# RG-LRU branch of a hybrid decoder block: convolution read from PSUM, gelu projections ahead of the gates, weights rounded on ScalarE

## The chip, the cores and the metric

One core of one Trainium2 chip runs the whole kernel. The metric is device time in microseconds (us) of one execution; less is better. Engines are called PE (TensorE), DVE (VectorE), ACT (ScalarE), POOL (GpSimd) and SP (SyncE, which issues DMAs). PEld is PE's weight load.

## The reference

A decoder block over 512 tokens plus 16 learned meta tokens (528 in all), width 1024, float32. Cut to what matters here, it is:

```python
proj = rmsnorm(h, norm1_g) @ w_in            # columns for q, f, i, og, lx, ly, ga, gb
o_a = hgrn2_branch(q_pre, f_pre, i_pre, og_pre, lb, hg_norm_g)

# rglru_branch(lx, ly, ...), 1024 channels in 8 blocks of 128
xc = causal_depthwise_conv(lx, conv_w, width=4) + conv_b
r = sigmoid(xc_block @ w_r[block] + b_r)
i = sigmoid(xc_block @ w_i[block] + b_i)
log_a = -8 * r * softplus(-lam)
u = sqrt(-expm1(2 * log_a)) * (i * xc)
h_t = exp(log_a_t) * h_{t-1} + u_t           # scan over the tokens
o_b = h * gelu(ly)

merged = sigmoid(ga) * (o_a @ w_up_a) + sigmoid(gb) * (o_b @ w_up_b)
h = h + merged @ w_out
h = h + hier_moe(rmsnorm(h))                 # 32 experts, top-1 group, top-2 in it
return rmsnorm(h)[:, 16:]
```

The four taps of the convolution run over tokens: output token t takes lx of t, t-1, t-2 and t-3.

## The kernel before, in words

Channels lie on partitions and tokens along the free dimension. Every dense product is made of three matmuls of rounded operands: a float32 operand is split into a rounded high part (hi) and the rounded rest (lo), and the product is hi x hi + hi x lo + lo x hi. `split` (lines 85 to 90) does this: one engine copies with rounding (hi), another subtracts (lo).

**Weights.** The class `Weights` (lines 132 to 176) holds a queue of weight pieces in the order in which PE wants them (lines 178 to 193). A DMA of SP brings 256 columns (`raw`), `prep` rounds 128 of them into one of three buffers (`hl`), and `next` hands a piece to PE. Which engines round it is fixed where the piece is queued: for w_in's columns of lx (2048 on), ly (3072 on) and the gate blocks w_r and w_i, hi is made by DVE and lo by POOL; for the heads before it hi is made by ACT. `dense` (line 195) runs one projection in eight steps of k and calls `prep` in its middle for the piece after.

**The stage.** `lru` (line 619) goes over the eight blocks in four pairs. For a pair it projects lx for both blocks (`proj(True, ...)`, two PSUM tiles of 256 and 272 tokens each), and `use_lx` makes of each: two ACT copies from PSUM into `lxp` in SBUF (one buffer for all blocks), on DVE the fourth tap with the bias (line 639) and three more taps (line 641) into `xc`, then hi on ACT and lo on DVE into `xh` (one buffer). Then for each block of the pair `gates` (twelve matmuls into four PSUM tiles, tanh on ACT, products on DVE) and the block's ly projection with gelu (`use_ly`, into the tile `ge`, one buffer for both blocks of a pair).

**The finish.** `finish` of a pair (line 682: logarithms and exponentials on ACT, the scan over tokens and products on DVE, the rounding of o_b into `obH` on DVE and `obL` on POOL) is called after the next pair's lx projections; the last one is called at the end.

**What sets the order.** The program's text, then a scheduler that may hoist independent instructions on each engine; each engine then works through its own list in order and waits at the head of it. Eight PSUM banks are handed out by that scheduler as they come free. Beside the stage run the steps of the HGRN2 heads 2 and 3 (`hgrn_head`, one step after every fifth step of k): masks, exponentials and small matmuls. After the stage comes `merge` (line 788): for each of four column groups two gate projections (ga), two products with w_up_a, two gate projections (gb), two products with w_up_b, which need `obH` and `obL`; its weights are rounded by DVE and POOL. Buffers that come free in `merge` and after it start the DMAs of the expert weights (`prefetch`, line 747), which go on to the end.

Of the kernel before, what the change touches and what calls it, by code (L numbers as in the profile page):

```python
# [8 lines left out]
F32 = mybir.dt.float32  # L9
F32R = mybir.dt.float32r  # L10
# [4 lines left out]
AF = mybir.ActivationFunctionType  # L15
OP = mybir.AluOpType
# [4 lines left out]
N = T + M  # L21
D = 1024
KD = D // 128
# [5 lines left out]
EPS = 1e-6  # L29
BIG = 3.0e38  # L30
PARTS = ((0, 256), (256, 528))
NLATE = 10
EV1, EV2 = 2, 5
LEVELS = (64, 32, 16, 8, 4, 2, 1)
# [3 lines left out]
def hybrid_block_kernel(ctx: ExitStack, tc: tile.TileContext, x, meta, norm1_g, w_in, hg_lb,  # L38
# [37 lines left out]
    def ms(tag, shape, dtype, name):  # L76
        return misc.tile(shape, dtype, name=uniq(name), tag="m" + tag)

    def ps(shape, name, dtype=F32):
        return psum.tile(shape, dtype, name=name, tag="ps")  # L80
# [97 lines left out]
    W = Weights()  # L178
# [1 line left out]
        for base in (512, 0, 1024, 1536):  # L180
            W.columns(w_in2, base + 128 * h, ACT, POOL)
    for b in range(0, NB, 2):
        W.columns(w_in2, 2048 + 128 * b, DVE, POOL)
        W.blocks([w_r[0], w_i[0]], b, DVE, POOL)
        W.columns(w_in2, 3072 + 128 * b, DVE, POOL)
    for j in range(0, KD, 2):
        W.columns(w_in2, 4096 + 128 * j, DVE, POOL)
        if j:
# [6 lines left out]
    def dense(outs, cols_, nk, aH, aL):  # L195

        wh, wl = W.next()
        for k in range(nk):
            if k == nk // 2:
                W.prep()  # L200
            for w, a in ((wh, aH), (wh, aL), (wl, aH)):
                for o, (c0, c1) in zip(outs, cols_):
                    PE.matmul(o[:, :c1 - c0], w[:, k, :], hsl(a, k, c0, c1),  # L203
                              start=(k == 0 and w is wh and a is aH),
                              stop=(k == nk - 1 and w is wl))
            yield

    def proj(all_tokens, use):
        if all_tokens:
            pp = [ps([128, 272], "pj") for _ in PARTS]  # L210
            yield from dense(pp, PARTS, KD, hnH, hnL)
            use(pp)
        else:
            p_ = ps([128, 512], "pj")
            yield from dense([p_], [(M, N)], KD, hnH, hnL)
            use(p_)
# [119 lines left out]
    def col(nm, i=None):  # L336
        a, b = R[nm]
        return cols[:, a:b] if i is None else cols[:, a + i:a + i + 1]
# [278 lines left out]
        add_slots(late, [f"t{i}" for i in range(NLATE)])  # L617

    def lru():
        MX = ms("F", [128, 2, 3 + N], F32, "lxi")  # L620
        lxp, iv = MX[:, 0], MX[:, 1, :N]
        L2 = ms("G", [128, 2, N], F32, "l2")
        DVE.memset(lxp[:, :3], 0.0)
        tail = None
        for b0 in range(0, NB, 2):
            bs = (b0, b0 + 1)
            XC = ms("AH"[b0 // 2 % 2], [128, 2, N], F32, "xc")
            RR = ms("C", [128, 2, N], F32, "r")
            TH = ms("D", [128, 2, N], F32, "th")
            GE = ms("E", [128, 2, T], F32, "ge")  # L630
            XH = {}
            WG = []

            def use_lx(b):
                def f(pp):
                    for (a, c), p_ in zip(PARTS, pp):
                        ACT.activation(lxp[:, 3 + a:3 + c], p_[:, :c - a], AF.Copy)
                    xc = XC[:, b - b0]
                    DVE.tensor_scalar(xc, lxp[:, 3:], col("cw", 24 + b), col("cb", b), op0=OP.mult, op1=OP.add)
                    for w in range(3):  # L640
                        DVE.scalar_tensor_tensor(xc, lxp[:, w:w + N], col("cw", 8 * w + b), xc,  # L641
                                                 op0=OP.mult, op1=OP.add)
                    xh = XH[b] = ms("B", [128, 2, N], F32R, "xh")
                    split(xh[:, 0], xh[:, 1], xc, ACT, DVE)
                return f

            def gates(b):
                xh, i = XH[b], b - b0
                r, th = RR[:, i], TH[:, i]
                for gi, dst in enumerate((r, iv)):  # L650
                    pg = [ps([128, 272], "pg") for _ in PARTS]
                    for w, a in ((0, 0), (0, 1), (1, 0)):
                        for (c0, c1), p_ in zip(PARTS, pg):
                            PE.matmul(p_[:, :c1 - c0], WG[w][:, 2 * gi + i], xh[:, a, c0:c1], start=(w == 0 and a == 0), stop=(w == 1))
                    for (c0, c1), p_ in zip(PARTS, pg):
                        ACT.activation(dst[:, c0:c1], p_[:, :c1 - c0], AF.Tanh, scale=0.5, bias=hb[:, 8 * gi + b:8 * gi + b + 1])
                ACT.activation(th, r, AF.Tanh, scale=C4[:, b:b + 1], bias=C4[:, b:b + 1])
                DVE.scalar_tensor_tensor(XC[:, i], iv, 1.0, XC[:, i], op0=OP.add, op1=OP.mult)
                DVE.tensor_scalar(th, th, 2.0 ** -60, None, op0=OP.max)

            def use_ly(b):
                def f(p_):

                    c, ge = math.sqrt(2 / math.pi), GE[:, b - b0]
                    ACT.activation(ge, p_, AF.Square)
                    DVE.tensor_scalar(ge, ge, 0.044715 * c, c, op0=OP.mult, op1=OP.add)
                    DVE.tensor_mul(ge, ge, p_)
                    ACT.activation(ge, ge, AF.Tanh)
                    DVE.scalar_tensor_tensor(ge, ge, 1.0, p_, op0=OP.add, op1=OP.mult)
                return f  # L670

            for b in bs:
                yield from proj(True, use_lx(b))
            if tail:
                tail()
            WG += W.next()
            for b in bs:
                gates(b)
                W.prep()
                yield  # L680
                yield from proj(False, use_ly(b))
            def finish(b0=b0, bs=bs, XC=XC, RR=RR, TH=TH, GE=GE):
                for i in range(2):
                    ACT.activation(L2[:, i], TH[:, i], AF.Ln, bias=1.0)
                    ACT.activation(TH[:, i], TH[:, i], AF.Ln, scale=2.0)
                    DVE.tensor_sub(TH[:, i], TH[:, i], L2[:, i])
                if b0 == 4:
                    end_heads()
                    add_ob()
                for i, b in enumerate(bs):  # L690

                    av, u, ge = RR[:, i], TH[:, i], GE[:, i]
                    ACT.activation(av, av, AF.Exp, scale=NC4[:, b:b + 1], bias=NC4[:, b:b + 1])
                    ACT.activation(u, u, AF.Exp, scale=0.5, bias=nln2)
                    DVE.tensor_mul(u, u, XC[:, i])
                    DVE.tensor_tensor_scan(u, av, u, 0.0, op0=OP.mult, op1=OP.add)
                    DVE.scalar_tensor_tensor(ge, ge, 0.5, u[:, M:], op0=OP.mult, op1=OP.mult)
                    split(obH[b // 4][:, b % 4], obL[b // 4][:, b % 4], ge, DVE, POOL)

            tail = finish  # L700
        tail()
# [558 lines left out]
```

## Time and profile before

| what | value |
|---|---|
| median of 3 runs | 1007.72 us (1007.44 to 1009.9) |
| the profiled execution, its own time | 1008.98 us |
| its span | 1007.3 us |
| the stage of the four pairs (first lx matmul to last ly matmul) | 140.9 to 296.3 us of the span |
| `merge` up to its last weights | 296.3 to about 480 us |
| expert weights at full rate | about 562 to 977 us, 408 GB/s |

The rows in the next section but one are read as follows. A row by line and engine gives busy time and the mean of one instruction, then the idle time of the engine in front of them and what ended it. [...]

### The profile page before, as it was taken

The page shows a single profiled execution, that of the slowest core. Times are in us where ns is not written, and L with a number is a line of the kernel's source. Part 1 is how long each engine was busy: PE and PEld are TensorE (multiplying, and loading weights), DVE is VectorE, ACT ScalarE, POOL GpSimd, SP SyncE. Part 2 cuts the span into 40 slices and gives each one's busy share as a digit, 9 for nine tenths or more (in the row PEclk, how much of TensorE's full clock was granted, in tenths as well). Part 3 has the DMA queues.
Part 4 walks back from the last instruction along what each step waited for, and adds up shares of the span by engine and source line. Part 5 has one row for each costly group of instructions (what it writes and reads, how often), then busy time and mean ns, then how long its engine had stood idle before and what let it go on. Part 6 is the DMA issues. An engine that isn't in the chain of part 4 may idle for free.

```text
span 1007.3 us, 12273 instructions
## 1 busy us (share of the span) xinstructions
PE 937.2 (93%) x4812; PEld 603.6 (60%) x4812; DVE 503.5 (50%) x951; ACT 241.6 (24%) x440; POOL 248.0 (25%) x167
## 2 busy tenths in 40 slices
PE   7989999897799999999959999999999999999984
PEld 5979998887678888888733444434334343433331
DVE  5678569997986434352542333333333343333323
ACT  6445526464472000000401010101101010110104
POOL 4543442253456454444300000000000000000002
PEclk9999999998989999999959999999999999999998
DMA  6221120220256231317978999999999999999992
GB/s 213 81 89 42 44 94 13 83 94 11 84 213 248 89 126 63 126 63 274 374 282 311 410 409 408 408 408 408 409 409 408 409 408 408 408 408 409 408 360 86
DMA packets 94297, 251.76 MB, mean 250 GB/s; under 512 B 6581, under 2 KB 39433, under 8 KB 94234
## 3 DMA queue, kind: packets, MB, share of 16 engines
q1 hardware_dynamic: 91352, 244.61, 63.5%
q0 software_dynamic: 2304, 4.20, 1.1%
q10 hardware_dynamic: 578, 2.10, 0.5%
q8 instruction: 40, 0.66, 0.3%
q14 instruction: 23, 0.19, 0.1%
HBM read 250.89 MB, written 4.19 MB: 253 GB/s over the span
## 4 chain that ended last, share of the span: by engine, by line
PE 62%; DMA 4%; DVE 4%; issue 1%; ACT 0%; POOL 0%; SPq 0%; POOLq 0%; DVEq 0%; ACTq 0%
PE pj L203 15%; PE put L998 11%; PE py L1017 10%; PE pgt L998 10%; PE pcb L1031 6%; DMA wx<-in_w_up_dram 4%; PE po L783 3%; PE pw L960 2%; PE pxs L990 1%; PE po L1055 1%; DVE xc L641 1%; PE pht L1011 1%; DMA XG<-HD,idx 1%; DVE HG L1004 1%; PE pT L886 0%
## 5 line engine op out<-in xcount | busy, mean ns | idle before, releaser
L203 PE MATMUL pj<-hnH,hl 128*128 128x512 f32 (+1 forms) x960 | 251.1, 351 | 4.2 <-POOL hl L90 3.9
L90 POOL TENSOR_TENSOR hl<-raw,hl 128x1024 fp32r<-128x1024 f32 (+1 forms) x76 | 174.0, 2291 | 202.8 <-DVE hl L89 138.2
L203 PEld LDWEIGHTS pj<-hnH,hl 128*128 128x128 f32 x960 | 162.9, 191 | 28.6 <-POOL hl L90 5.6
L203 PE MATMUL pj<-hnL,hl 128*128 128x512 f32 (+1 forms) x480 | 148.5, 347 | 0.0
L1034 DVE TENSOR_TENSOR h<-h,pcb 128x512 f32<-128x512 f32 x124 | 77.6, 683 | 109.8 <-PE pcb L1031 109.8
L998 PE MATMUL put<-wx,XS 128*64 128x512 f32 x512 | 120.2, 600 | 2.0 <-DMA wx<-in_w_up_dram 2.0
L998 PE MATMUL pgt<-wx,XS 128*64 128x512 f32 x512 | 117.9, 605 | 1.3 <-DMA wx<-in_w_gate_dram 1.2
L967 POOL DMA_INDIRECT XG<-HD,idx x16 | 16.5, 1029 | 409.0 <-DVE sw L976 250.5
L1017 PE MATMUL py<-wx,HG 128*64 128x512 f32 x512 | 115.5, 603 | 0.7 <-ACT HG L1012 0.7
L89 DVE CAST hl<-raw 128x1024 fp32r<-128x1024 f32 (+1 forms) x60 | 50.2, 837 | 86.6 <-PE pj L203 76.9
L203 PEld LDWEIGHTS pj<-hnL,hl 128*128 128x128 f32 x480 | 84.6, 191 | 10.2
L998 PEld LDWEIGHTS pgt<-wx,XS 128*64 128x64 f32 x512 | 36.0, 139 | 70.5 <-issue 64.6
L1017 PEld LDWEIGHTS py<-wx,HG 128*64 128x64 f32 x512 | 35.5, 138 | 67.5 <-issue 63.6
L998 PEld LDWEIGHTS put<-wx,XS 128*64 128x64 f32 x512 | 33.3, 136 | 65.8 <-issue 62.0
L1025 DVE SCALAR_TENSOR_TENSOR Y<-py,sw,Y 128x512 fp32r<-128x512 f32 x31 | 23.3, 751 | 93.3 <-ACT Y L1024 92.3
L1031 PE MATMUL pcb<-Y,OHT 128*128 128x512 f32 x248 | 68.1, 411 | 0.0
L1031 PEld LDWEIGHTS pcb<-Y,OHT 128*128 128x128 f32 x248 | 43.5, 188 | 39.3 <-issue 30.8
L1012 ACT ACTIVATE HG<-pht 128x512 f32<-128x512 f32 x16 | 9.6, 598 | 182.9 <-PE pht L1011 182.8
L1024 ACT ACTIVATE Y<-py,sw 128x512 fp32r<-128x512 f32 x31 | 21.3, 688 | 104.2 <-PE py L1017 104.2
L203 PE MATMUL pj<-obH,hl 128*128 128x512 f32 x128 | 40.1, 389 | 0.0
L1003 ACT ACTIVATE HG<-pgt,sw 128x512 f32<-128x512 f32 x16 | 11.0, 688 | 106.4 <-PE pgt L998 106.4
L950 DVE TENSOR_TENSOR OHI<-iota,RK 128x128 f32<-128x128 f32 x64 | 15.7, 286 | 39.3 <-PE pw L960 39.1
(263 smaller groups left out, 1161.7 us busy)
## 6 DMA issues: line engine op xcount, KB each, us to landing
wx<-in_w_up_dram SPq DMA_DIRECT2D x64, 1024.0 KB, 18.3
wx<-in_w_gate_dram SPq DMA_DIRECT2D x62, 1024.0 KB, 18.4
wx<-in_w_down_dram SPq DMA_DIRECT2D x60, 1024.0 KB, 19.0
raw<-in_w_in_dram SPq DMA_DIRECT2D x24, 1024.0 KB, 5.3
raw<-in_w_up_b_dram SPq DMA_DIRECT2D x4, 1024.0 KB
raw<-in_w_out_dram SPq DMA_DIRECT2D x4, 1024.0 KB
wx<-in_w_down_dram SPq DMA_DIRECT2D x8, 512.0 KB, 17.2
h<-in_x_dram SPq DMA_DIRECT2D x2, 1024.0 KB
```

What stands on the lines that cost most here:

```text
L89: he.tensor_copy(hi, src)
L90: le.tensor_sub(lo, src, hi.bitcast(F32))
L203: PE.matmul(o[:, :c1 - c0], w[:, k, :], hsl(a, k, c0, c1), start=(k == 0 and w is wh and a is aH), stop=(k == nk - 1 and w is wl))
L783: PE.matmul(p_, mg[:, a, k, 128 * t:128 * t + 128], w[:, k, :], start=(k == 0 and a == 0 and w is wh), stop=(k == 1 and a == 1))
L960: PE.matmul(pw[:, :n], oh[:, t], tab[:, t], start=(t == 0), stop=(t == 3))
L967: POOL.indirect_dma_start(XG, None, HD[:], bass.IndirectOffsetOnAxis(ap=idx, axis=0), bounds_check=T - 1, oob_is_err=False)
L998: PE.matmul(p_[CAP * e:CAP * e + CAP], XS[:, k, CAP * e:CAP * e + CAP], weight(w2, e, k, 0), start=(k == 0), stop=(k == 7))
L1017: PE.matmul(p_[CAP * e:CAP * e + CAP], HT[:, 128 * k + CAP * e:128 * k + CAP * e + CAP], weight(w2, e, k, 512 * half), start=(k == 0), sto ...
L1024: ACT.activation(yh, p_, AF.Copy, scale=sw[:, 0:1])
L1025: DVE.scalar_tensor_tensor(Y[half][:, 1], p_, sw[:, 0:1], yh.bitcast(F32), op0=OP.mult, op1=OP.subtract)
L1031: PE.matmul(p_, oht[:, 128 * t:128 * t + 128], Y[half][:, i], start=(i == 0), stop=(i == 1))
L1034: DVE.tensor_add(hs, hs, p_)
```

## The change

Five edits, all in or for the stage.

1. **The convolution reads PSUM.** `lxp` is gone. ACT makes the fourth tap with its bias straight from PSUM into `xc` (Identity with scale and bias columns), and DVE adds the other three taps, each in two halves that read the two PSUM tiles. For that the second tile holds four tokens more (252 to 528, `PARTS4`), so that it has the tokens in front of token 256.
2. **ly ahead of the gates.** A pair now runs lx, lx, ly, ly, gates, gates.
3. **Two buffers of `xh`**, one for each block of the pair (tags B and G).
4. **The weights of the stage** (lx, ly, gate blocks) are rounded to hi by ACT, as those of the heads were; the pieces stand in the queue in the new order.
5. The tile of the second gate, `iv`, is now the first half of `L2`, a scratch tile of `finish`.

```diff
+PARTS4 = ((0, 256), (252, 528))
...
     for b in range(0, NB, 2):
-        W.columns(w_in2, 2048 + 128 * b, DVE, POOL)
-        W.blocks([w_r[0], w_i[0]], b, DVE, POOL)
-        W.columns(w_in2, 3072 + 128 * b, DVE, POOL)
+        W.columns(w_in2, 2048 + 128 * b, ACT, POOL)
+        W.columns(w_in2, 3072 + 128 * b, ACT, POOL)
+        W.blocks([w_r[0], w_i[0]], b, ACT, POOL)
...
-    def proj(all_tokens, use):
+    def proj(all_tokens, use, parts=PARTS):
         if all_tokens:
-            pp = [ps([128, 272], "pj") for _ in PARTS]
-            yield from dense(pp, PARTS, KD, hnH, hnL)
+            pp = [ps([128, b - a], "pj") for a, b in parts]
+            yield from dense(pp, parts, KD, hnH, hnL)
...
-        MX = ms("F", [128, 2, 3 + N], F32, "lxi")
-        lxp, iv = MX[:, 0], MX[:, 1, :N]
-        L2 = ms("G", [128, 2, N], F32, "l2")
-        DVE.memset(lxp[:, :3], 0.0)
+        L2 = ms("F", [128, 2, N], F32, "l2")
+        iv = L2[:, 0]
...
                 def f(pp):
+                    xc = XC[:, b - b0]
                     for (a, c), p_ in zip(PARTS, pp):
-                        ACT.activation(lxp[:, 3 + a:3 + c], p_[:, :c - a], AF.Copy)
-                    xc = XC[:, b - b0]
-                    DVE.tensor_scalar(xc, lxp[:, 3:], col("cw", 24 + b), col("cb", b), op0=OP.mult, op1=OP.add)
-                    for w in range(3):
-                        DVE.scalar_tensor_tensor(xc, lxp[:, w:w + N], col("cw", 8 * w + b), xc,
-                                                 op0=OP.mult, op1=OP.add)
-                    xh = XH[b] = ms("B", [128, 2, N], F32R, "xh")
+                        ACT.activation(xc[:, a:c], p_[:, p_.shape[1] - (c - a):], AF.Identity,
+                                       scale=col("cw", 24 + b), bias=col("cb", b))
+                    for d in range(1, 4):
+                        for (a, c), p_ in zip(PARTS, pp):
+                            n = p_.shape[1]
+                            o = xc[:, max(a, d):c]
+                            DVE.scalar_tensor_tensor(o, p_[:, n - d - o.shape[1]:n - d], col("cw", 8 * (3 - d) + b), o,
+                                                     op0=OP.mult, op1=OP.add)
+                    xh = XH[b] = ms("BG"[b - b0], [128, 2, N], F32R, "xh")
                     split(xh[:, 0], xh[:, 1], xc, ACT, DVE)
...
             for b in bs:
-                yield from proj(True, use_lx(b))
+                yield from proj(True, use_lx(b), PARTS4)
             if tail:
                 tail()
+            for b in bs:
+                yield from proj(False, use_ly(b))
             WG += W.next()
+            W.prep()
             for b in bs:
                 gates(b)
-                W.prep()
                 yield
-                yield from proj(False, use_ly(b))
```

Where the edits move instructions is shown at three places. Names: `l` and `l2` are the scratch of the finish, `th` and `r` its tiles, `e` an exponential of the heads, `hl_...` a piece of weights, `xh` the rounded `xc`, `ge` the gelu tile, `pj` a projection's and `pg` a gate's PSUM tile. Line numbers of the changed kernel are a few higher.

ACT in the second pair, from the logarithms of the first pair's finish on. Before:

```order
L684 ACT_TABLE_LOAD
L684 ACTIVATE l_76_1461<-th_1465 128x528 [waits DVE_49]
L665 ACTIVATE ge_1466<-pj 128x512 [waits PE_49]
L685 ACTIVATE th_1465<-th_1465 128x528 [waits Activation_49]
L473 ACT_TABLE_LOAD
L473 ACTIVATE e_1816<-e_1816 128x512 [waits DVE_49]
L668 ACTIVATE ge_1466<-ge_1466 128x512 [waits DVE_49]
L694 ACTIVATE th_1465<-th_1465,nln_390 128x528 [waits DVE_49]
L473 ACTIVATE e_1877<-e_1877 128x512 [waits DVE_49]
L637 ACTIVATE lxi_1460<-pj 128x256 [waits PE_49]
L637 ACTIVATE lxi_1460<-pj 128x272 [waits PE_49]
```

Of the change:

```order
L689 ACT_TABLE_LOAD
L689 ACTIVATE th_1462<-th_1462 128x528 [waits Activation_49]
L688 ACTIVATE l_75_1459<-th_1462 128x528
L697 ACT_TABLE_LOAD
L697 ACTIVATE r_1461<-r_1461,spt 128x528
L689 ACT_TABLE_LOAD
L689 ACTIVATE th_1462<-th_1462 128x528 [waits Activation_49]
L88 ACTIVATE xh_1904<-xc_1822 128x528 [waits DVE_49]
L697 ACT_TABLE_LOAD
L697 ACTIVATE r_1461<-r_1461,spt 128x528
L88 ACTIVATE hl_2054<-raw_1758 128x1024 [waits Pool_49]
```

Before, the finish of the first pair was through ACT ahead of the second pair's first lx copy (L637); now nearly all of it stands behind that pair's first convolution (these rows come after its two taps of L638), with four table loads in these eleven rows (two before) and six from the first logarithm of the finish on, and the rounding of a weight piece (`hl_2054`) stands behind them.

ACT further on in the second pair, from the second block's taps to its first gelu. Before, the square that starts the gelu (L665) with what is around it:

```order
L87 ACTIVATE xh_2002<-xc_1826 128x528 [waits DVE_49]
L684 ACT_TABLE_LOAD
L684 ACTIVATE l_76_1461<-th_1828 128x528 [waits DVE_49]
L665 ACTIVATE ge_1829<-pj 128x512 [waits PE_49,Pool_49]
L685 ACTIVATE th_1828<-th_1828 128x528 [waits Activation_49]
```

Of the change, where that square is L668:

```order
L638 ACTIVATE xc_1822<-pj,cols 128x256 [waits PE_49]
L638 ACTIVATE xc_1822<-pj,cols 128x272 [waits PE_49]
L88 ACTIVATE hl_2098<-raw_1953 128x512 [waits DMAHW2_49,DMAHW1_49,Pool_49]
L88 ACTIVATE xh_2003<-xc_1822 128x528 [waits DVE_49,Activation_49]
L88 ACTIVATE hl_2127<-raw_2057 128x1024 [waits DMAHW3_49,PE_49,Pool_49]
L668 ACTIVATE ge_1825<-pj 128x512 [waits Pool_49]
L478 ACTIVATE e_2050<-e_2050 128x256 [waits DVE_49]
L671 ACTIVATE ge_1825<-ge_1825 128x512 [waits DVE_49]
L668 ACTIVATE ge_1825<-pj 128x512 [waits PE_49]
L659 ACTIVATE r_1823<-pg,hb 128x256 [waits PE_49]
```

The square still waits for POOL (the last reader of the first pair's `ge`), and now all tanh of the pair's gates (L659) stand behind it.

POOL at the end of the stage and the start of `merge`. Before (`hl_2792` is the first piece of gb):

```order
L90 TENSOR_TENSOR hl_2731<-raw_2631,hl_2731 128x512 [waits DMAHW5_49,DVE_49]
L90 TENSOR_TENSOR obL_2677<-ge_2521,obH_2676 128x512 [waits DVE_49]
L90 TENSOR_TENSOR hl_2776<-raw_2631,hl_2776 128x512 [waits DVE_49]
L90 TENSOR_TENSOR obL_2677<-ge_2521,obH_2676 128x512 [waits DVE_49]
L90 TENSOR_TENSOR hl_2792<-raw_2734,hl_2792 128x1024 [waits DMAHW0_49,DVE_49]
```

Of the change (`hl_2925` is the same piece):

```order
L91 TENSOR_TENSOR hl_2854<-raw_2709,hl_2854 128x1024 [waits DVE_49]
L91 TENSOR_TENSOR hl_2883<-raw_2764,hl_2883 128x512 [waits DMAHW5_49,DVE_49,Pool_49]
L91 TENSOR_TENSOR hl_2908<-raw_2764,hl_2908 128x512 [waits DVE_49]
L91 TENSOR_TENSOR obL_2678<-ge_2517,obH_2677 128x512 [waits DVE_49] x2
L91 TENSOR_TENSOR hl_2925<-raw_2886,hl_2925 128x1024 [waits DMAHW0_49,DVE_49,PE_49]
```

The order of this piece behind the last pair's `obL` is the same; what has moved is the pair's ly projections, which PE now does ahead of the gates and no longer between the last gates and `merge`.

## Rows read from the trace of the kernel before

**Rows 1.** The page's busy time and share of the span by engine.

```profile
PE 937.2 (93%) x4812; PEld 603.6 (60%) x4812; DVE 503.5 (50%) x951; ACT 241.6 (24%) x440; POOL 248.0 (25%) x167
```

**Rows 2.** Windows, after the stage: `merge`, then the expert weights.

```profile
296.30:480.00 183.70, 183.70 (x802) 150.16 (x801) 83.61 (x105) 21.44 (x32) 92.61 (x46) 1.00 0.42 148
562.00:977.00 415.00, 402.48 (x1890) 168.90 (x1887) 148.33 (x318) 37.25 (x56) 13.16 (x13) 1.00 1.03 408
```

**Rows 3.** Windows, one for each pair of blocks: PE, PEld, DVE, ACT, POOL busy, clock.

```profile
140.90:174.40 33.50, 32.44 (x217) 29.19 (x216) 26.00 (x40) 16.90 (x34) 11.39 (x6) 1.00 0.21 69
174.40:215.40 41.00, 35.71 (x232) 31.71 (x231) 41.00 (x70) 22.43 (x38) 17.84 (x8) 0.96 0.19 59
215.40:257.30 41.90, 36.13 (x235) 33.25 (x234) 35.65 (x45) 22.09 (x43) 15.72 (x9) 0.92 0.18 57
257.30:296.30 39.00, 30.97 (x180) 27.36 (x179) 35.16 (x40) 22.30 (x44) 19.23 (x11) 0.87 0.41 149
```

**Rows 4.** Waits of PE in the stage, 140.9 to 296.3 us.

```profile
PE pg L654 <- ACT xh L87: 13.4, 4, 6.9
PE pj L203 <- POOL hl L90: 3.0, 2, 2.3
```

**Rows 5.** Windows, the three stretches of PE work at the low clock.

```profile
208.40:212.00 3.60, 3.56 (x9) 2.81 (x10) 3.60 (x9) 1.93 (x5) 1.11 (x1) 0.53 0.25 73
236.40:242.60 6.20, 5.35 (x18) 4.56 (x19) 6.07 (x6) 3.56 (x9) 3.42 (x2) 0.50 0.05 15
277.20:283.30 6.10, 6.02 (x19) 5.18 (x20) 6.02 (x7) 4.47 (x10) 5.26 (x4) 0.50 0.40 141
```

**Rows 6.** Lines of DVE in the stage: roundings of weights, taps of the convolution.

```profile
L641 DVE SCALAR_TENSOR_TENSOR xc<-lxi,cols,xc 128x528 f32<-128x528 f32 x24 | 27.1, 1129 | 0.4
L89 DVE CAST hl<-raw 128x1024 fp32r<-128x1024 f32 (+1 forms) x20 | 17.0, 848 | 3.0 <-PE pj L203 2.9
L639 DVE TENSOR_SCALAR xc<-lxi,cols 128x528 f32<-128x528 f32 x8 | 8.1, 1009 | 0.0
```

**Rows 7.** Single instructions by tile (xc, ge, st), ns min/median/max.

```profile
L641 DVE SCALAR_TENSOR_TENSOR xc<-lxi,cols,xc x24: 732/762/2794, 148.9 to 287.0; 128x528 f32<-128x528 f32 x24
L669 DVE SCALAR_TENSOR_TENSOR ge<-ge,pj x8: 660/675/689, 176.1 to 303.4; 128x512 f32<-128x512 f32 x8
L552 DVE SCALAR_TENSOR_TENSOR st<-st,gend,pS x6: 331/333/336, 177.6 to 204.7; 128x128 f32<-128x128 f32 x6
```

**Rows 8.** Timelines of POOL and DVE around 252 us: start, us.

```profile
252.04 2.39 POOL L90 TENSOR_TENSOR hl<-raw,hl 128x1024 fp32r<-128x1024 f32 x1
...
252.10 0.69 DVE L573 TENSOR_TENSOR on<-po,rs 128x512 f32<-128x512 f32 x1 [2.35 <-POOL rs L106]
252.71 2.00 DVE L666 TENSOR_SCALAR ge<-ge 128x512 f32<-128x512 f32 x1
```

**Rows 9.** Lines of ACT: copies and tanh from PSUM, roundings, gelu's square, table loads.

```profile
L637 ACT ACTIVATE lxi<-pj 128x256 f32<-128x256 f32 (+1 forms) x16 | 5.3, 379 | 6.4 <-PE pj L203 6.4
L656 ACT ACTIVATE lxi<-pg,hb 128x256 f32<-128x256 f32 (+1 forms) x16 | 7.1, 480 | 0.9 <-PE pg L654 0.9
L87 ACT ACTIVATE hl<-raw 128x1024 fp32r<-128x1024 f32 x16 | 16.7, 1051 | 5.8 <-PE pj L310 3.1 <-PE pc L333 1.9 <-PE pj L203 0.7
L665 ACT ACTIVATE ge<-pj 128x512 f32<-128x512 f32 x7 | 4.1, 584 | 0.7 <-POOL obL L90 0.7
L684 ACT ACT_TABLE_LOAD x7 | 9.0, 1283 | 0.1
```

**Rows 10.** The chain that ended last, around the end of the stage.

```profile
289.22 1.48 PE pg L654 x10
290.70 55.47 PE pj L203 x240
```

**Rows 11.** Timeline of POOL, end of the last pair's finish.

```profile
308.64 1.67 POOL L90 TENSOR_TENSOR obL<-ge,obH 128x512 fp32r<-128x512 f32 x1 [2.45 <-DVE obH L89]
310.27 5.25 POOL L90 TENSOR_TENSOR hl<-raw,hl 128x1024 fp32r<-128x1024 f32 x2
```

## The prediction

> **What bounds the kernel now.** I read the page's busy time first: PE is at 93% of the span, the other engines at 50% or less [rows 1], so time can only be won where PE waits or runs slowly. The windows then say where. In `merge` PE is busy in 183.70 of 183.70 us, and the expert weights after it run at 408 GB/s, with the DMA engines full [rows 2]. Their transfers start when buffers of `merge` come free. So neither hides anything: if the stage of the four pairs ends 10 us sooner, all that follows starts 10 us sooner, and the end moves one for one. Inside the stage PE is not full: 135.25 us busy (32.44 + 35.71 + 36.13 + 30.97) of 155.4 [rows 3]. In the second pair DVE is busy in all of its 41.00 us, and in the next two it works for 35 of 39 to 42. PE's waits name the same place: 13.4 us at the first gate matmuls for `xh`, the end of the chain ACT copy, four taps, rounding, and 3.0 us for pieces of weights [rows 4]. [...] At half speed half of the busy time is lost: 3.56 x 0.47 = 1.67, 5.35 / 2 = 2.68 and 6.02 / 2 = 3.01, 7.4 us together.
>
> So **the most that the change can give** is 155.4 less PE's work at full clock, 135.25 - 7.4 = 127.9, plus the four columns more of each lx matmul on the second tile (8 blocks x 24 matmuls = 192; 0.231 us for 512 columns [rows 10], so 192 x 4/512 x 0.231 = 0.35): 27.2 us.
>
> **The change, part by part.**
>
> *Roundings from DVE to ACT.* DVE loses 20 casts, 17.0 us [rows 6]. ACT takes 20 at up to 1.051 us [rows 9], 21.0 at most. Its load is 83.7 us of 155.4 [rows 3], so there is room; what matters is where they stand in its queue (below). POOL still makes each lo; its order follows the new queue of pieces, and so does SP's. SP's DMAs are the same in number and size, and with shares of 0.18 to 0.41 [rows 3] their order costs nothing; that cover is gone only in a stage with full queues.
>
> *The convolution.* Gone from DVE: 24 taps (27.1 us) and 8 fourth taps (8.1 us) [rows 6], 35.2 us or 4.40 a block. New: 48 half taps of about 264 columns from PSUM, which no row shows. The rows around it are 0.333 us for 128 columns and 0.675 for 512, both from PSUM [rows 7]; on the line between them 264 columns take 0.454, so 21.8 us. Ends: 0.348 (0.675 x 264/512), 16.7 us, and 0.675, 32.4 us. I take 0.454, between two rows of the same operation, and a saving of 13.4 us (2.8 to 18.5). ACT makes 16 taps at 0.480 (the form with scale and bias, [rows 9]) for 16 copies at 0.379: +1.6. DVE comes to 137.8 - 17.0 - 13.4 = 107, ACT to 106.
>
> The old taps took 732 ns at best and 2794 at worst [rows 7]. While POOL ran for 2.39 us, a DVE instruction with SBUF operands alone took 2.00 us, and one that reads PSUM beside it its usual 0.69 [rows 8]; all eight PSUM rows of line 669 lie within 660 to 689 [rows 7]. Taps that read PSUM should therefore not be held up by POOL. [...]
>
> *ly ahead of the gates, two `xh`.* The first gates of a pair now have two ly projections, 2 x 24 x 0.231 = 11.1 us [rows 10], in front of them while `xc` is made and rounded (six taps, 2.7 us, and two roundings). The 13.4 us of [rows 4] go, with most of the low clock behind them. The second `xh` lets the second block's rounding start without waiting for the first block's gates. PSUM banks stay with DVE for some 2 us longer than with the copies; nothing of PE's next work uses those banks, so I cost this at nothing.
>
> *What is late next.* A gate of the second block takes the bank that the first ly projection held, and that bank is free only after the first block's gelu. Its square on ACT waits for POOL, for the last reader of the one `ge` buffer, `obL` of the pair before (the second order place). So a pair's second gates now wait for the finish of the pair before. Unobstructed, that finish took from the last gates' end at 290.70 [rows 10] to 308.64 + 1.67 = 310.3 [rows 11], 19.6 us. In the second pair more lies in its way: on ACT three table loads more than there (3 x 1.283), three weight roundings (3 x 1.051) and four taps (4 x 0.480) [rows 9]; on DVE two convolutions with their lo (2 x 3.4); on POOL one lo of weights (2.4, [rows 8]). In series this is 18.2; partly side by side I take 16. `obL` then ends 35 to 36 us after the pair's start, and the gelu (0.58 on ACT [rows 9], three DVE steps of 0.4 to 0.7 and a tanh, 3 in all) gives the bank at 38 to 39. PE has 35.71 - 1.67 = 34.0 us of work in this pair [rows 3, 5], and wants the bank one block's gates (1.4) and part of the heads' work before its end, at 31 to 32: **a wait of 7 us**, and the clock behind it, as in the 6.02 us at half clock [rows 5], 2.8. Behind the held square all tanh of this pair's gates stand on ACT, which PE feels as the same wait.
>
> *Smaller waits.* The second ly's weights are rounded on ACT behind four table loads (first order place): 1 us. The third pair has two loads and the same chain, 0.5; the fourth has POOL's `obL` of the third, 1.5. At the hand-over, `merge` needs the first piece of gb, whose lo stands on POOL behind the last `obL` (third order place): 19.6 + 2.4 = 22.0 us after the last gates. Before, PE had a ly projection (5.55), two ga (11.1) and the two products with w_up_a (2 x 2.8) to do: 22.2, no wait. Now the ly is done before: 16.7. The wait is up to 5.3; with a finish that DVE no longer delays by casts I take 3, plus 1.0 of low clock.
>
> **The sum.** 27.2 - (7 + 2.8 + 1 + 0.5 + 1.5 + 3 + 1.0 = 16.8) = 10.4, from which I take 0.2 for the four taps that PE sees at the start of the first pair. The profiled execution's own 1008.98 becomes 998.8; the median of 1007.72, 1.26 lower, becomes **997.5 us**. The kernel's measurement can tell about 0.3% (3 us) from no change.
>
> **The rivals.**
> 1. *The late bank is not felt.* If the finish keeps its 19.6 us to within 10, the square runs in time, and what stays is 1 to 7 us: a gain of 20 to 25, 983 to 988. For it: DVE has 30 us less to do in the stage, and it was full in the second pair. Against: the six table loads there.
> 2. *ACT's queue holds the weights.* If in the second to fourth pair a rounding of weights comes later by one table load (1.28) and PE falls to the low clock for it (2.7), that is up to 12 us more than the forecast: 1003 to 1009. For it: 5.8 us of idle ACT time stand in front of its roundings of the heads already [rows 9]. Against: pieces are asked for half a projection ahead, 2.8 us.
> 3. *Slower.* If the bank comes as late in all of the last three pairs as in the second, that is 3 x 9.8 = 29.4, and with 4 at the hand-over 33.4, more than the 27.2: about 1014. The point is 5 us of wait a pair, (27.2 - 4)/3 - 2.8. Against: the third and the fourth pair have two table loads each, not six.
> 4. *The taps from PSUM are held as those from SBUF were.* The convolution keeps 4.40 us a block and the finish in the second pair comes 2 x 1.7 later: 3.4 to 4.5, so 1001 to 1002. [...] Against it: [rows 7, 8].
> 5. *Nothing moves the end*, 1008, if the experts' transfers were started by something other than `merge`. Against: [rows 2].
>
> **The numbers.** Forecast (989 to 1003) 0.52; first rival 0.20; second 0.13; third 0.08; fourth 0.05; fifth 0.02. Likeliest is a partial gain, so 997.5. The range is 985 to 1006: it leaves out the better third of the first rival, the worse third of the second, the third and the fifth, about 0.2 together. The unknown half tap, at its ends, moves the second pair's finish by -1.3 to +2.7, well inside. Faster by over 0.3% is below 1004.7: forecast, first and fourth rival and a third of the second, 0.81. Within 0.3%: the most of the second, the fifth, and a mild third rival, 0.13. Slower: 0.06.
>
> **What would show it.** Right: no wait of PE's first gates for ACT's `xh`; half taps of about 0.45 us, none over 0.7; a wait of about 7 us of PE's gate in the second pair for DVE's last step of `ge`, and a square on ACT that waits for POOL's `obL`; PE at 0.5 of the clock behind it; a short wait for POOL's `hl` early in `merge`; the stage some 10 us shorter and the rest of the span as long as before. Wrong: half taps stretched like the old ones (fourth rival), PE's waits for `hl` in every pair (second), no such wait (first), or a wait of over 5 us in each pair (third). A stage that shrinks while the time stays would refute the first paragraph.

## The result, and the profile after

The changed kernel takes **1017.22 us** (median of 4 runs, 1015.91 to 1017.96) against 1008.49 us before (4 runs): ratio 1.0085, 95% interval [1.0073, 1.0098]. It is slower by 0.85%. The forecast was 997.5 with a range of 985 to 1006, so the prediction was wrong in sign.

The profiled execution's span went from 1007.3 to 1016.3 us. First the windows of the changed kernel, one for each pair of blocks, then the hand-over to `merge` and the rest of `merge` (columns as in [rows 3]: PE, PEld, DVE, ACT, POOL busy, granted clock of PE with 1.00 as the full one, DMA share, GB/s).

```profile
140.90:174.70 33.80, 33.80 (x230) 30.85 (x228) 23.68 (x49) 15.69 (x31) 9.14 (x5) 1.00 0.22 70
174.70:218.00 43.30, 35.42 (x229) 32.27 (x229) 36.15 (x66) 30.39 (x47) 14.15 (x7) 0.92 0.17 55
218.00:262.00 44.00, 36.47 (x236) 33.62 (x235) 31.77 (x38) 24.74 (x52) 18.50 (x10) 0.89 0.19 61
262.00:306.00 44.00, 38.01 (x210) 33.87 (x209) 31.26 (x45) 28.91 (x48) 19.82 (x11) 0.88 0.47 174
306.00:330.00 24.00, 20.40 (x81) 15.95 (x80) 15.41 (x23) 5.52 (x8) 13.38 (x6) 0.93 0.55 191
330.00:480.00 150.00, 150.00 (x649) 121.61 (x649) 48.66 (x72) 11.01 (x18) 74.83 (x36) 1.00 0.31 105
```

The first pair is what was hoped for: PE is busy in all of its 33.80 us at full clock. In the next three PE works 35 to 38 us in 43 to 44, at 0.92, 0.89 and 0.88 of the clock. The waits of PE in the stage and at the hand-over (engine, line, what it waited for: us in total, times, longest) answer to [rows 4]:

```profile
PE pg L657 <- DVE ge L672: 10.8, 3, 6.0
PE pg L657 <- DVE sc L559: 5.4, 1, 5.4
PE pj L204 <- POOL hl L91: 3.4, 2, 3.1
PE pj L204 <- ACT r L659: 2.5, 1, 2.5
PE pg L657 <- DVE on L574: 2.0, 1, 2.0
```

The wait for `xh` (13.4 us before) is gone. In its place stand waits of the gates for PSUM banks that VectorE has not freed: the last step of `ge`, and steps of the heads (`sc`, `on`) that stand in its list. Once (2.5 us) a projection waits for a bank that ScalarE's tanh of the gates (`r`) has not freed. By place, in PE's timeline (start, us, instruction, idle time in front and its releaser):

```profile
211.90 1.45 PE L657 MATMUL pg<-xh,hl 128*128 128x272 f32 x5 [5.41 <-DVE sc L559]
215.06 3.01 PE L657 MATMUL pg<-xh,hl 128*128 128x256 f32 x12 [1.72 <-DVE ge L672]
254.25 0.89 PE L657 MATMUL pg<-xh,hl 128*128 128x272 f32 x5 [3.07 <-DVE ge L672]
257.13 1.69 PE L657 MATMUL pg<-xh,hl 128*128 128x256 f32 x6 [2.00 <-DVE on L574]
261.28 0.58 PE L204 MATMUL pj<-hnH,hl 128*128 128x256 f32 x1 [2.46 <-ACT r L659]
295.39 1.69 PE L657 MATMUL pg<-xh,hl 128*128 128x256 f32 x6 [5.99 <-DVE ge L672]
319.11 0.73 PE L204 MATMUL pj<-hnH,hl 128*128 128x512 f32 x2 [3.09 <-POOL hl L91]
```

Some 7 us stand in the second pair, 7.5 in the third, 6.0 in the fourth, 3.1 at the hand-over (3.6 with a short wait before it). After these waits PE runs slowly; the stretches of it in the second, third and fourth pair and at the hand-over, answering to [rows 5]:

```profile
211.90:221.10 9.20, 7.48 (x33) 7.17 (x34) 6.44 (x16) 7.79 (x15) 0.57 (x1) 0.51 0.00 0
254.20:265.80 11.60, 7.09 (x33) 6.57 (x34) 6.74 (x8) 8.37 (x19) 3.38 (x2) 0.56 0.08 23
295.30:299.80 4.50, 4.41 (x14) 3.79 (x15) 4.47 (x6) 3.76 (x10) 3.02 (x2) 0.54 0.30 98
319.10:323.40 4.30, 4.29 (x12) 3.39 (x13) 0.51 (x1) 0.00 (x0) 4.30 (x2) 0.60 0.08 16
```

Summed as the prediction summed the stretches before, I estimate the loss at 7.48 x 0.49 + 7.09 x 0.44 + 4.41 x 0.46 + 4.29 x 0.40 = 10.5 us, against 7.4 before. (From the mean clock of the whole windows it is 12.8 against 8.4, but these means also count time in which PE waits.) The first expert product (`pgt`) starts 8.4 us later than before, of the 9.0 that the span grew: what the stage and the hand-over lose moves all that follows, as the first paragraph of the prediction had it. Before and after:

```profile
L998 PE MATMUL pgt<-wx,XS x512: 592/592/1116, 524.7 to 962.6; 128*64 128x512 f32 x171
L1002 PE MATMUL pgt<-wx,XS x512: 592/592/1116, 533.1 to 971.9; 128*64 128x512 f32 x171
```

### The profile page after: what moved, and what is told of

Its sections match the earlier page's. It is cut to its first block, busy times and chain, and to the rows that moved or that the text cites. A ratio compares the mean times of both kernels' runs of the same rounds, so it can differ in the third digit from the quotient of the medians.

```text
span 1016.3 us, 12312 instructions
## 1 busy us (share of the span) xinstructions
PE 940.8 (93%) x4812; PEld 606.5 (60%) x4812; DVE 466.0 (46%) x946; ACT 255.1 (25%) x456; POOL 244.7 (24%) x167
## 4 chain that ended last, share of the span: by engine, by line
PE 75%; DVE 10%; ACT 5%; DMA 5%; POOL 2%; issue 2%; SPq 0%; POOLq 0%; DVEq 0%; ACTq 0%
PE pj L204 24%; PE put L1002 11%; PE pgt L1002 10%; PE py L1021 10%; PE pcb L1035 6%; DMA wx<-in_w_up_dram 4%; PE po L787 3%; PE pl L543 2%; PE pw L964 2%; PE pxs L994 1%; PE po L1059 1%; POOL hl L91 1%; PE pht L1015 1%; DVE th L700 1%; DVE ge L669 1%
## 5 line engine op out<-in xcount | busy, mean ns | idle before, releaser
L204 PEld LDWEIGHTS pj<-hnH,hl 128*128 128x128 f32 x960 | 164.9, 193 | 31.8 <-POOL hl L91 5.7
L90 DVE CAST hl<-raw 128x1024 fp32r<-128x1024 f32 (+1 forms) x40 | 31.0, 776 | 61.3 <-PE pj L204 59.6
L88 ACT ACTIVATE hl<-raw 128x1024 fp32r<-128x1024 f32 (+1 forms) x36 | 35.9, 1006 | 7.4 <-PE pj L311 3.2
```

Of the source, the lines that this page charges most:

```text
L88: ACT.activation(hi, src, AF.Copy)
L90: he.tensor_copy(hi, src)
L204: PE.matmul(o[:, :c1 - c0], w[:, k, :], hsl(a, k, c0, c1), start=(k == 0 and w is wh and a is aH), stop=(k == nk - 1 and w is wl))
```

## The experiments

The theory, formed from these traces: in the new order both blocks' gates come last, so a pair's whole finish falls into the next pair, and on VectorE that pair's gelu stands behind it; the gates wait for the banks that the gelu holds. The rivals: ScalarE's roundings hold up the finish; or the loads of DVE and POOL bind in any order. In each experiment below, the median of the kernel before in the same session was 1009.05 to 1009.65 us.

**order_back**: the order and the queue of weights as before, the rest of the change kept.

```diff
-            for b in bs:
-                yield from proj(False, use_ly(b))
             WG += W.next()
-            W.prep()
             for b in bs:
                 gates(b)
+                W.prep()
                 yield
+                yield from proj(False, use_ly(b))
```

> The changed kernel with only its order undone: gates before ly again, the weight pieces queued in that order, everything else of the change kept (taps from PSUM, two xh, weights rounded on ScalarE). Theory (the order makes the finish of a pair one lump in the next pair, and the one ge buffer ties the second gates to its end): the waits of the gates for the last step of ge (10.8 us) and those of the banks behind it go, a shorter wait for xh comes back (before: 13.4 us in 4), and the time is 996 to 1004, below the kernel before. Rival one (the weight roundings on ScalarE hold up the finish): 1012 or more. Rival two (the loads of DVE and POOL bind, whatever the order): 1010 to 1017.

Measured: 998.7 us, ratio 0.9892 [0.9874, 0.9909], as the theory had it. Beside the rest of the change the order costs 18.5 us, and the rest without it gains 10. Both rivals fall as the whole cause.

**conv_xh_only** and **conv_only**: order and weights (`DVE` in the queue) as before; the second without the second `xh`. Both keep the fifth edit, the move of `iv`. The line by which the second differs from the first:

```diff
-                    xh = XH[b] = ms("BG"[b - b0], [128, 2, N], F32R, "xh")
+                    xh = XH[b] = ms("B", [128, 2, N], F32R, "xh")
```

> The kernel before with only the convolution from PSUM and the two xh buffers: order and weights as before. Theory: DVE's chain to xh is some 2 to 5 us shorter in each pair, the waits for xh fall from 13.4 to about 5: 997 to 1004. If it is no faster than 1007, the convolution was not what PE waited for.

> The kernel before with only the convolution from PSUM; one xh, order and weights as before. Theory: the convolution makes the gain of the run with both (997.3), and the second xh is worth 0 to 3 us in the old order, where the first block's gates come early: 997 to 1001. If the second xh made the gain: 1004 to 1009.

Measured: 997.34 (0.9882 [0.9866, 0.9898]) and **996.84 us** (0.9876 [0.9859, 0.9892]), the two fastest kernels of this study. All of the gain comes with the convolution; the second `xh` is worth nothing in the old order. The taps in conv_only (ns min/median/max, answering to [rows 7]), and what is left of PE's waits there for `xh`:

```profile
L644 DVE SCALAR_TENSOR_TENSOR xc<-pj,cols,xc x48: 465/483/501, 148.6 to 270.8; 128x272 f32<-128x272 f32 x24, 128x255 f32<-128x255 f32 x8, 128x254 f32<-128x254 f32 x8, 128x253 f32<-128x253 f32 x8
```

```profile
PE pg L657 <- ACT xh L88: 4.0, 1, 4.0
PE pg L657 <- DVE xh L91: 2.3, 2, 2.0
```

VectorE's taps take some 23.2 us (48 x 0.483) for 35.2 before [rows 6]. Of these 12.0 us, 8.1 are the fourth taps, which ScalarE now makes; the three others go from 27.1 to 23.2. No run changes one of the two without the other.

**order_only**: the kernel before with the new order alone (the first diff turned round).

> The kernel before with only the order changed: ly ahead of the gates, the weight pieces queued so; taps from SBUF, one xh, weights on DVE. Theory: the order costs by itself, 14 to 18 us as between the runs with it and without it, so 1020 to 1030. Rival (the order costs only together with the new convolution): 1005 to 1012.

Measured: 1012.83 us, 1.0041 [1.0027, 1.0056]. It costs by itself, but 3.5 us, not 14 to 18: a miss on the size. PE still waits 10.8 us for `xh` there:

```profile
PE pg L654 <- ACT xh L87: 10.8, 3, 5.8
```

In the new order these waits are no longer those of a pair's first gates. All three stand in front of the second block's gates, whose `xh` goes into the one buffer that the first block's gates have just read, as in the fourth pair:

```profile
288.28 1.98 PE L654 MATMUL pg<-xh,hl 128*128 128x256 f32 x8 [0.64 <-POOL hl L90]
296.06 1.25 PE L654 MATMUL pg<-xh,hl 128*128 128x256 f32 x4 [5.79 <-ACT xh L87]
```

So the parts don't add: the order costs 3.5 us beside the old convolution with one `xh`, and 14.5 beside the new one with two (w_dve against conv_xh_only).

**w_dve**: the new order, roundings on VectorE (`DVE` for `ACT` in the three queue lines).

> The changed kernel with the stage's weights rounded on VectorE again, the new order kept. Theory: the finish is still one lump in the next pair, DVE has 17 us more to do and ScalarE 17 to 21 less, so 1013 to 1021 with waits of the gates for ge in all of the last three pairs. Rival one (ScalarE's roundings hold up the finish): 1000 to 1008, those waits halved.

Measured: 1011.82 us, 1.0021 [1.001, 1.0032], between the two and 1.2 us below the theory's range: some 5 us of the loss come with ScalarE's roundings, 14.5 don't.

**ge_two**: two `ge` buffers (and nine late buffers instead of ten, `NLATE = 9`, for the room).

```diff
-            GE = ms("E", [128, 2, T], F32, "ge")
+            GE = ms("EI"[b0 // 2 % 2], [128, 2, T], F32, "ge")
```

> The changed kernel with two ge buffers, used by the pairs in turn; the room for it comes from one of the ten late buffers of the expert weights (nine are left). Theory: the gelu no longer waits for the finish of the pair before, the waits of the gates for ge go (10.8 us, with the low clock behind them some 5 more), and the stage ends 10 to 20 us sooner: 998 to 1007, if nine late buffers cost nothing. If ge is only one of several ties (r and th have one buffer too), waits for tanh take its place and the time is 1008 to 1014. Rival two (loads of DVE and POOL bind): 1014 or more.

Measured: 1017.0 us, 1.0079 [1.006, 1.0098]: no gain, and the theory in that form falls. In the second pair PE's waits stay what they were (5.4 for `sc`, 1.7 for `ge`), and the timelines show why. In the changed kernel ScalarE's square waited for POOL, as the prediction had it, and DVE took the result at 211.66:

```profile
210.83 0.60 ACT L668 ACTIVATE ge<-pj 128x512 f32<-128x512 f32 x1 [6.67 <-POOL obL L91]
```

```profile
211.66 0.41 DVE L669 TENSOR_SCALAR ge<-ge 128x512 f32<-128x512 f32 x1
```

With two buffers the square runs ten us sooner, and DVE takes it at the same time as before:

```profile
201.00 0.58 ACT L668 ACTIVATE ge<-pj 128x512 f32<-128x512 f32 x1
```

```profile
204.74 0.68 DVE L701 SCALAR_TENSOR_TENSOR ge<-ge,th 128x512 f32<-128x512 f32 x1
205.34 0.34 DVE L553 SCALAR_TENSOR_TENSOR st<-st,gend,pS 128x128 f32<-128x128 f32 x1
205.60 1.23 DVE L90 CAST obH<-ge 128x512 fp32r<-128x512 f32 x1
206.76 2.56 DVE L488 TENSOR_TENSOR z<-kk,e 128x256 f32<-128x256 f32 x1
209.24 1.48 DVE L491 TENSOR_TENSOR z<-qT,e 128x256 f32<-128x256 f32 x1
...
211.30 0.41 DVE L669 TENSOR_SCALAR ge<-ge 128x512 f32<-128x512 f32 x1
```

In DVE's list the gelu's first step (L669) stands behind the finish (L701, `obH`) and behind steps of the heads, and it ran after them, 9.7 us after the square's end. In the fourth pair the second buffer does help: the wait for `ge` falls from 6.0 to 1.6 us. But a piece of weights then costs 1.6 and the hand-over 6.4 instead of 3.6, so the experts start only 1.2 us sooner (531.9).

**gelu_first**: ge_two, with the finish called behind the ly projections, which puts gelu steps ahead of finish steps in that list. (It moves the finish in ScalarE's list too.)

```diff
-            if tail:
-                tail()
             for b in bs:
                 yield from proj(False, use_ly(b))
+            if tail:
+                tail()
```

> The run with two ge buffers (and nine late buffers), with the finish called behind the ly projections, so that on VectorE the first steps of the gelu stand ahead of the last steps of the finish. Theory (with two ge buffers it was VectorE's own list that kept the gelu behind the finish): the waits of the gates for ge fall from 6.3 us to under 2 and the time to 1009 to 1014; the finish is as late as before, so the hand-over and the waits for tanh stay. Rival (the order on VectorE does not matter, only its load): 1016 to 1018 as in that run.

Measured: 1000.14 us, 0.991 [0.9888, 0.9932]: 17 us less than ge_two by the place of the finish alone, and 9 below the range that I expected. L669 now runs at 199.46, between the steps of the finish, and PE's waits are down to these:

```profile
199.46 0.42 DVE L669 TENSOR_SCALAR ge<-ge 128x512 f32<-128x512 f32 x1
199.79 1.25 DVE L700 TENSOR_TENSOR_SCAN th<-r,th 128x528 f32<-128x528 f32 x1
```

```profile
PE pj L204 <- POOL hl L91: 6.6, 2, 4.8
PE pj L204 <- ACT r L659: 3.1, 1, 3.1
PE pg L657 <- DVE ge L672: 1.4, 1, 1.4
PE pg L657 <- ACT l L659: 0.9, 1, 0.9
```

ScalarE's list changed with VectorE's: between 176 and 200 us it has four table loads there, six in ge_two, and it rounds the second block's `xc` at 196.40 instead of 200.44. How much of the 17 us each list gives is not separated. The last gates start at 274.2 instead of 296.7 us. Whether one `ge` buffer would do could not be tried: the gelu can't be written ahead of the finish that still reads it.

**finish_first**: the changed kernel, with the finish ahead of the next pair's lx projections.

```diff
+            if tail:
+                tail()
             for b in bs:
                 yield from proj(True, use_lx(b), PARTS4)
-            if tail:
-                tail()
```

> The changed kernel with one thing moved: the finish of a pair is called ahead of the next pair's lx projections, so that on ScalarE and DVE its steps stand in front of the next convolution and of the next gelu. The new order, the one ge buffer and the weights on ScalarE stay. Theory (what the second gates wait for is a late finish, stretched between the next pair's taps and roundings, and the gelu that stands behind it on DVE): obL ends some 20 us after the pair's start instead of 29 to 37, the waits of the gates for ge go, and with the hand-over's 3 to 5 us left the time is 995 to 1003. Rival (the order itself costs, wherever the finish stands, since both blocks' gates come last): 1010 or more.

Measured: 1008.75 us, 0.9997 [0.9985, 1.0008], between the theory's range and the rival's. The waits for `ge` go and the last gates start 11.5 us sooner (285.2), but at the hand-over 6.4 us are lost, and a rounding on ScalarE behind the finish costs 2.9 in the second pair:

```profile
185.45 0.81 PE L204 MATMUL pj<-hnH,hl 128*128 128x256 f32 x2 [2.90 <-ACT hl L88]
```

```profile
303.69 0.47 PE L204 MATMUL pj<-hnH,hl 128*128 128x512 f32 x1 [1.64 <-DVE hl L90]
309.16 1.22 PE L204 MATMUL pj<-hnH,hl 128*128 128x512 f32 x2 [4.76 <-POOL hl L91]
```

**old_order_finish_first**: the same move in conv_xh_only.

> The run with convolution from PSUM, two xh, old order and old weights, with the finish called ahead of the next pair's lx projections. Theory: the finish was not late in the old order, since its first block is through before the pair ends; 994 to 1000, within 3 us of 997.3; slower if the taps now stand behind the finish on DVE and the first gates wait for xh (then up to 1005).

Measured: 1010.55 us, 1.0005 [0.9991, 1.002], a miss by 10 us on the theory and 5.5 above its slower case: the taps now stand behind and between the finish's steps on VectorE, and the first gates wait for `xh` again (10.2 us). A finish moved forward cost some 13 us here, where the taps on that list are awaited sooner.

**last_pair_old**, **finish_first_last_old**, **gelu_first_last_old**: the old order in the last pair alone (`old = b0 == NB - 2`, and the last pieces of the queue in their old order), in the changed kernel, in finish_first and in gelu_first.

> The changed kernel with the old order (gates ahead of ly) in the last pair alone. Theory (at the hand-over the merge has one ly projection less to cover the last finish, and in the last pair the second gates wait 6.0 us for ge): both go, 3.6 us of waits for hl and 6.0 for ge with 3 to 4 us of low clock; part of it comes back as a wait for xh (3 to 4): 1004 to 1010. Rival (the last pair's order is not what costs): 1014 or more.

> The changed kernel with the finish called ahead of the next pair's lx projections, and the old order in the last pair. Theory: with the late finish and the hand-over both mended, what the new order costs is gone but for the small waits: 997 to 1003 (1008.75 of the run with the finish first, less 6.4 us of waits at the hand-over and about 2 of low clock). Rival (something else in the new order costs): 1006 or more.

> The run gelu_first with the old order in the last pair alone, so that merge again has a ly projection in front of the first gb weights. Theory (4.8 us of wait and about 2 of low clock at the hand-over are what the new order still costs there): 993 to 998. If the last pair's first gates then wait as long for xh (6.7 us in the run finish_first_last_old), nothing is won: 999 to 1003.

Measured: 1020.44 (1.0102 [1.0083, 1.012]), 1007.35 (0.998 [0.9968, 0.9991]) and 1001.47 us (0.993 [0.9911, 0.995]). The first two miss; the third is the case where nothing is won. In each the wait at the hand-over shrinks or stays, and waits in the last pair take its place, as this one of finish_first_last_old:

```profile
PE pg L660 <- ACT xh L88: 6.7, 1, 6.7
```

So the hand-over is a wait that can be read off, but it isn't shown to be a price of the order that this edit gives back.

**finish_first_last_old_dve**, **gelu_first_dve**: the roundings on VectorE in those kernels. **conv_two_ge**: conv_only with two `ge` buffers.

> The run with the finish first and the old order in the last pair, with the stage's weights rounded on VectorE as before. Theory (the roundings on ScalarE are worth 1 us or less once the finish is early): 996 to 1003, within 2 us of the same kernel with the roundings on ScalarE. If VectorE, which now does the finish and the casts ahead of the taps, is too full: 1004 to 1010.

> The run gelu_first with the stage's weights rounded on VectorE as before. Theory (ScalarE's roundings cost or save little where the finish is not waited for): 998 to 1003. If VectorE's 17 us of casts between the finish and the gelu delay the gates again: 1004 or more.

> The run conv_only (old order, 996.84) with two ge buffers in the room that the scratch tile left. Theory (in the old order the gelu was late only by 0.7 us, so ge binds nothing): 995 to 999, no change beyond 2 us.

Measured: 1007.84 (0.9982 [0.9971, 0.9994]), 1006.14 (0.9964 [0.9949, 0.9978]) and 998.16 us (0.9899 [0.9878, 0.992]). The first misses its range, though the roundings differ by under 2 us as expected; the second comes out as its slower case; the third as expected. The roundings on ScalarE are worth nothing in the first and 6.0 us in the second, and cost 5.4 in the changed kernel; in the old order order_back and conv_xh_only differ by 1.4, within the noise. That this depends on which list holds what PE wants next is my reading; no run isolates it. Two `ge` buffers give nothing in the old order.

## Why the prediction was wrong, step by step

- **What bounds the kernel** was right: PE's waits in the stage and the low clock behind them, passed on nearly one for one (the first expert product 8.4 us later, the span 9.0 longer). Of the three slow stretches of [rows 5], from which the 7.4 us in the forecast's 27.2 are worked out, two begin where waits of 2.32 and 5.00 us end, the third (277.20) where the longest wait of [rows 4], 6.9 us, ends:

```profile
208.44 1.20 PE L203 MATMUL pj<-hnH,hl 128*128 128x512 f32 x2 [2.32 <-POOL hl L90]
236.48 0.81 PE L654 MATMUL pg<-xh,hl 128*128 128x256 f32 x2 [5.00 <-ACT xh L87]
```

- **The convolution** was right. A half tap takes 0.483 us at the median in conv_only as in the changed kernel (forecast 0.454, so 23.2 us for 48, not 21.8), and the longest 0.501 and 0.502. Six taps of the changed kernel with POOL at work beside them take 2.47 us, no more than six with POOL idle (2.48 at 184.20), so the fourth rival is out:

```profile
279.19 2.47 DVE L644 SCALAR_TENSOR_TENSOR xc<-pj,cols,xc 128x255 f32<-128x255 f32 x6
```

```profile
278.66 1.76 POOL L91 TENSOR_TENSOR oaL<-o,oaH 128x512 fp32r<-128x512 f32 x1
280.39 1.29 POOL L91 TENSOR_TENSOR hl<-raw,hl 128x512 fp32r<-128x512 f32 x1
```

The convolution from PSUM was the better one here: conv_only is 1.24% faster than the kernel with the copies, though the larger part of what VectorE saves (8.1 of 12.0 us) is the fourth tap that ScalarE took over.
- **The second pair** was right in place and size, in part by luck. The finish's last `obL` ended 36.8 us after the gates (210.8 - 174.0; forecast 35 to 36), the wait was 7.1 (forecast 7). But 5.4 of it ended with `sc`, a step of the heads behind the finish in VectorE's list, and only 1.7 with `ge`, which alone was named. The one `ge` buffer holds the square and VectorE's list holds the next step; ge_two shows that here the list alone is enough (square at 201.00 instead of 210.83, next step at 211.30 instead of 211.66).
- **The step that failed** is "the third pair has two loads and the same chain, 0.5; the fourth has POOL's obL of the third, 1.5". They measured 7.5 and 6.0. I took the six table loads for what makes the second pair long and did not walk the chain of the other two. There too the finish shares its engines with two convolutions, roundings and POOL: in the third pair it ran from 218.1 to 248.5, 30.4 us, and in the fourth from 258.8 to 290.7, 31.8, for 19.6 unobstructed. In the third pair on VectorE the finish lay around the second block's taps, and steps with SBUF operands took longer beside POOL's lo than with POOL idle, L661 2.60 us for 0.70 (at 215.99) and L662 2.62 for 0.43 (at 216.60):

```profile
220.89 2.60 DVE L661 SCALAR_TENSOR_TENSOR xc<-l,xc 128x528 f32<-128x528 f32 x1
223.41 2.62 DVE L662 TENSOR_SCALAR th<-th 128x528 f32<-128x528 f32 x1
...
238.84 2.46 DVE L644 SCALAR_TENSOR_TENSOR xc<-pj,cols,xc 128x255 f32<-128x255 f32 x6
241.21 2.39 DVE L700 TENSOR_TENSOR_SCAN th<-r,th 128x528 f32<-128x528 f32 x2
```

```profile
220.53 5.22 POOL L91 TENSOR_TENSOR hl<-raw,hl 128x1024 fp32r<-128x1024 f32 x2 [9.73 <-PE pl L543]
```

The finish is not all of the third pair's 7.5 us. The first 3.1 end with the gelu whose square came behind `obL`. But ahead of each block's gelu VectorE also waited for POOL's `rs` of the heads (the first time behind that `obL`), and the gelu's first step took 1.99 and 2.47 us beside POOL's roundings (249.43 and 256.82 us, 2.38 and 2.36 long), for 0.41 at 211.66 with POOL idle. How much each of these costs stays open:

```profile
249.49 0.69 DVE L574 TENSOR_TENSOR on<-po,rs 128x512 f32<-128x512 f32 x1 [3.41 <-POOL rs L107]
250.10 1.99 DVE L669 TENSOR_SCALAR ge<-ge 128x512 f32<-128x512 f32 x1
...
256.39 0.69 DVE L574 TENSOR_TENSOR on<-po,rs 128x512 f32<-128x512 f32 x1 [2.19 <-POOL rs L107]
257.00 2.47 DVE L669 TENSOR_SCALAR ge<-ge 128x512 f32<-128x512 f32 x1
```

- **The low clock** was mis-sized with it: 2.8 + 1.0 forecast, about 10.5 estimated from the slow stretches, as there are four of them, not two.
- **The hand-over** was right: 3.6 us (forecast 3).
- **The sum** with the measured terms: 27.2 - (25.0 of waits + 10.5) = -8.3, a loss; the experts start 8.4 us later, and the span lost 9.0. Of the 18.7 us between 35.5 and the forecast's 16.8, 11.5 are the waits of the third and fourth pair and 6.7 the low clock.
- **The rivals**: the third came, with waits of 7, 7.5 and 6 us a pair, above the 5 that it named. I gave it 0.08, for the count of table loads alone, when its own price list (19.6 us of finish, two convolutions, roundings, a lo on POOL) held for every pair.

## What to carry to other kernels

When work is moved ahead for one engine, walk the list of every engine that serves it, in every pair or iteration, not in the one that looks worst: here a free buffer was of no use while the next step stood behind others in VectorE's list (in ge_two the square ran 9.8 us sooner, that step 0.4). The second buffer gave nothing alone (1017.0 us for 1017.22); with the finish called later it came to 17 us. Each part of a change is worth testing alone: the convolution by itself was 1.2% faster, and the order put with it took that and more away.

## What the runs showed that I had not expected

Matmuls of `merge` that the change does not touch got a little longer in the kernels with the new convolution: `po` takes 396 ns at the median in the changed kernel and 394 in conv_only, against 389 before and in order_only. Over the first to the last of them that is 1.3 us (353.7 to 464.7 against 346.0 to 455.7). Why was not tried.

```profile
L787 PE MATMUL po<-hl,mg x144: 392/396/397, 353.7 to 464.7; 128*128 128x512 f32 x144
```
